# The gated half of the mixers' output projection computed among keys and values, its sums kept in DRAM, the S5 half added in a second pass

## The chip, the core and the metric

The kernel runs on one core of one Trainium2 chip. Its engines work side by side, each through an in-order queue of its own: PE multiplies matrices (PEld loads its weights), DVE and POOL do elementwise work, ACT does copies, casts and functions, and SP issues the DMAs. The metric is the device time of one execution in microseconds (us); lower is better. Everything below is fp32; a product of two fp32 matrices is made of three passes over a high and a low part of each operand.

## What is computed

The reference is one decoder layer on 1024 tokens of width 1024. Its first sub-layer has two mixers whose outputs are laid side by side and go through one output projection, `w_out`; a cross-attention into 256 memory tokens follows:

```python
h = rmsnorm(x, g_mix_pre[l])
s_in, s_gate, g_u, g_vv = jnp.split(h @ w_in[l], splits, axis=-1)
y_ssm = s5_ssm(s_in, ...)
y_ssm = jax.nn.gelu(y_ssm) * jax.nn.sigmoid(s_gate)
y_gmlp = chunked_spatial_gate(g_u, g_vv, g_v[l], w_s[l], b_s[l])
mix = jnp.concatenate([y_ssm, y_gmlp], axis=-1) @ w_out[l]
x = x + rmsnorm(mix, g_mix_post[l])
h = rmsnorm(x, g_x_pre[l])
mem_n = rmsnorm(mem, g_mem[l])
xa = memory_cross_attention(h, mem_n, w_q[l], w_k[l], w_v[l], w_o[l])
```

The S5 mixer (`y_ssm`, rows 0 to 511 of `w_out`) is a scan over time. The gated mixer (`y_gmlp`, rows 512 to 1023) has none and is finished earlier. Keys and values need only the memory tokens. A gated convolutional FFN comes after the attention; the change does not touch it.

## The kernel before

**Tiles.** Activations are held transposed: 128 features on the partitions, and the tokens in two halves `h` of 512. `self.mix[k, h]` is the mixers' output, k = 0 to 3 the S5 half and k = 4 to 7 the gated half; each is a pair of tiles, the high part (a cast by ACT) and the low part (a subtraction by DVE or POOL, `split`, L253/L254). `mm3` (L228) makes one product: for each k-tile three matmuls, high by high, high by low, low by high (all on L234).

**Weights.** A `Stream` holds all weight chunks (128x512, 256 KB) in the order of use. A chunk is loaded into one of 4 `raw` slots (L86), cast by ACT (L132), and its low part is subtracted by DVE (L135); the pair lies in `w`, which has 13 slots, so that some six chunks lie ready ahead of PE.

**The S5 stage.** In `mixers`, the S5 chain runs as a side job beside the matmuls: eight batches, each a passage through PE, DVE, POOL and DMAs that ends in the matmuls of L616/L617, and then `s5_final`, which multiplies with the gate (L657) and splits into `mix[0..3, h]`. When the last batch is still running, PE has the keys (L1043, eight blocks of 24 matmuls 128x256, two weight chunks each) and the values (L1051, four blocks of 48 such matmuls, four chunks each).

**The output projection.** It opens `attention` (L1109): for each token half h and each of 8 output blocks b, `proj` multiplies all eight k-tiles, the gated ones first (24 matmuls 128x512, two weight chunks), ACT copies the sum from PSUM into an `m` tile (L1095), and `sumsq` adds its square (ACT L710, POOL L711). Every weight chunk of `w_out` is loaded and split twice, once for each half. Four PSUM banks, `acc`, take turns.

**What follows.** `post` normalises the eight blocks of a half: the mean square (PE L279, some ten small DVE operations), a broadcast of the factors (PE L306, ACT L309), then for each block the scaling on DVE (L728), the residual on POOL (L729), the high part on ACT (L734) and the low part on DVE (L735). Only then can the queries (`q_block`) use that half. `post` of half 0 runs as a side job beside the projection of half 1; with half 1's projection done, the queries of half 0 come at once. `s_sums`, another side job, prepares weights of the FFN by way of DRAM on POOL and DMAs.

**Order.** The program gives the order and the dependencies; a scheduler that estimates times orders the instructions of each engine when the kernel is built, and each engine then keeps to that order.

Of the kernel before, what the change touches and what calls it, by code (L numbers as in the profile page):

```python
# [19 lines left out]
ALU = mybir.AluOpType  # L20
AX = mybir.AxisListType

P = 128
# [9 lines left out]
W_AHEAD = 6  # L33
PAIR_AHEAD = 12
SUM_AHEAD = 5
ON_POOL = ((4, 16, 1), (164, 184, 2))

POST_A = 0.8
POST_2B = 1
S5_RATE = 1.5  # L40
WARM = 10
EARLY = 1
MIX_AT = 2
# [21 lines left out]
class Stream:  # L65
# [13 lines left out]
    def add(self, ap, pair=None, name=None):  # L79
        self.items.append((ap, pair, name))  # L80
        return len(self.items) - 1
# [71 lines left out]
class Builder:  # L153
# [658 lines left out]
    def prepare(self, cp, dp):  # L812
        nc, a = self.nc, self.a
        g = nc.gpsimd
        self.w = w = Stream(self)

        self.ids = ids = {}

        def add(key, b):
            return [w.add(a[key][b, j]) for j in range(a[key].shape[1])]  # L820

        ids["s01"] = add("w_s01", 0)
        ids["s"] = [add("w_s23", i) for i in range(2)]
        ids["sg"] = [add("w_sg", i) for i in range(4)]
        ids["gv"] = [add("w_gv", i) for i in range(2)]
        ids["gu"] = [add("w_gu", i) for i in range(4)]
        ids["k"] = [add("w_k", i) for i in range(8)]
        ids["v"] = [add("w_v", i) for i in range(4)]
        for n in ("o1", "q", "o2"):
            ids[n] = [[], []]  # L830
        for h in range(2):
            ids["o1"][h] = [add("w_out", i) for i in range(8)]
        for h in range(2):
            ids["q"][h] = [add("w_q", i) for i in range(8)]
            ids["o2"][h] = [add("w_o", i) for i in range(8)]
        ids["up"] = {}
        for i in range(NP):
            ids["up"][i] = [None, None]
        for i in range(NP + 1):
            for j, n in ((0, i), (1, i - 1)):  # L840
                if 0 <= n < NP:
                    ids["up"][n][j] = w.add(a["w_up"][n, j])
        up = {i: {f"{q + 1}{j + 1}": a["w_up"][i + NP * q, j] for q in range(2) for j in range(2)}
              for i in range(NP)}
        raws = {i: {"n": i} for i in up}
        for i in range(-1, NP):
            for d, name in TURN:
                if i + d in up:
                    ids["up"][i + d, name] = w.add(up[i + d], raws[i + d], name)


        self.ones = cp.tile([P, P], F32, name="ones")
        g.memset(self.ones, 1.0)
        first = cp.tile([P, 1], F32, name="first")
        nc.scalar.activation(first, self.ones[:, 0:1], AF.Identity)

        ps = self.bank("st")
        for _ in range(WARM):
            nc.tensor.matmul(ps[:, :P], lhsT=self.ones, rhs=self.ones, start=True, stop=True)
        gains = cp.tile([P, 7, 8], F32, name="gains")  # L860
        self.gain = {n: gains[:, i] for i, n in enumerate(GAINS)}
        self.xs = {}
        for kt in range(KT):
            for h in range(2):
                t = self.slot("m")
                nc.sync.dma_start(t, a["xT"][P * kt:P * kt + P, HALF * h:HALF * h + HALF])
                self.xs[kt, h] = t
                if h == 0 and kt % 2 == 0:
                    w.load_to(kt // 2 + 1)
                if h == 0 and kt == 0:  # L870
                    nc.sync.dma_start(gains, a["gains"])
        self.ident = cp.tile([P, P], F32, name="ident")
        make_identity(nc, self.ident)
        self.conv = cp.tile([P, 44, 4], F32, name="conv")
        self.gv = cp.tile([P, 4], F32, name="gv")

        dram = lambda n, shape: dp.tile(shape, F32, name=n)
        self.ud = [dram(f"ud{i}", [8, P, P]) for i in range(4)]
        self.kd = [dram(f"kd{i}", [240, 64]) for i in range(4)]
        self.yd = [dram(f"yd{i}", [8, 16, 8, P]) for i in range(4)]  # L880
        halves = lambda n, k: [[dram(f"{n}{i}{h}", [P, HALF]) for h in range(2)] for i in range(k)]
        self.gd = halves("gd", 4)
        self.x1d = halves("x1d", 8)
        self.x2d = halves("x2d", 8)
        self.fd = halves("fd", NP)
        self.sd = {n: [dram(f"sd{n}_{i}", [P, HALF]) for i in range(11)] for n in range(1, 5)}
        self.p1d = [dram(f"p1d{i}", [P, HALF]) for i in range(NP)]
        self.v0d = [dram(f"v0d{i}", [P, HALF]) for i in range(NP)]
        self.xg = [[], []]
        self.qscale = [None, None]  # L890
        self.ready = [False, False]
        self.mix = {}


    def mixers(self):
        nc, a, w, ids, xg = self.nc, self.a, self.w, self.ids, self.xg
        v, g = nc.vector, nc.gpsimd
# [4 lines left out]
        for kt in range(KT):  # L902
# [9 lines left out]
            for h in range(2):  # L912
                rh, rl = xg[h][kt]
                for b in range(2):
# [3 lines left out]
                    c = slice(256 * (kt % 2) + P * b, 256 * (kt % 2) + P * b + P)  # L918
# [8 lines left out]
        for b in range(2):  # L927
            for h in range(2):
                t = self.slot("x")
# [110 lines left out]

        memv = lambda k, c=slice(0, 256): tuple(t[:, k % 2, c] for t in self.memp[k // 2])
        self.kraw, self.vraw = [], {}
        for b in range(8):  # L1043
            part = self.blocks(ids["k"][b])
            ps = self.bank()[:, :256]
            self.mm3(ps, [(*part(k), *memv(k)) for k in range(8)], ticks=1)
            if b % 2 == 0:
                self.kraw.append(self.slot("m", shape=[P, 2, 256]))
            nc.scalar.copy(self.kraw[-1][:, b % 2], ps)
        for c in range(4):  # L1050
            part = self.blocks(ids["v"][c], 256)  # L1051
            for mt in range(2):
                ps = self.bank()[:, :256]
                self.mm3(ps, [(*memv(k, slice(P * mt, P * mt + P)), *part(k)) for k in range(8)], ticks=1)
                if c % 2 == 0:
                    self.vraw[mt, c // 2] = self.slot("m")
                nc.scalar.copy(self.vraw[mt, c // 2][:, 256 * (c % 2):256 * (c % 2) + 256], ps)
        self.memp = None
        self.drain(s5)

# [1 line left out]
    def attention(self):  # L1062
# [37 lines left out]

        m1 = [[None] * 8, [None] * 8]
        sq1 = [None, None]
        xres = lambda i, hh: a["xT"][P * i:P * i + P, HALF * hh:HALF * hh + HALF]
        post = [None, None]
        s_job = self.s_sums()
        kv = self.side(kv_parts(), 1)
        for h in range(2):
            for b in range(8):
                proj(lambda k, hh: self.mix[k, hh], "o1", m1, sq1, b, h, (4, 5, 6, 7, 0, 1, 2, 3))  # L1109
                if h == 0:  # L1110
                    next(s_job)
            for k in range(8):
                del self.mix[k, h]
            post[h] = self.post(m1[h], sq1[h], "g_mix_post", xres, h, "q", lambda i, hh: self.x1d[i][hh])
            if h == 0:
                self.drain(kv)
                self.side(post[0])
# [534 lines left out]
```

## Time and profile before

| | |
|---|---|
| median of 3 runs | 1344.74 us (1344.46 to 1349.69) |
| the profiled execution | 1350.66 us, its span 1348.9 us |
| PE busy | 1271.5 us, 94% of the span |
| DVE, POOL, ACT busy | 1072.2, 687.2, 627.9 us |
| mean granted clock of PE | 0.977 |
| keys and values | 265.00 to 331.08 us of the span |
| output projection of the mixers | 331.08 to some 420 us |

The profiled execution took 5.9 us more than the median; all times of single instructions come from it. In a timeline row the columns are start, length, engine, line of the code, operation, output and inputs, the count, and in brackets the idle time before it with what ended it. Line numbers are those of the kernel before; in the changed kernel the same lines stand 3 or 4 further down in the helpers (L135 is L138 there, L617 is L620, L728 is L731, L735 is L738).

### The profile page before, as it was taken

What the parts mean: (1) busy time and instruction counts of PE and PEld (TensorE: products, weight loads), DVE (VectorE), ACT (ScalarE), POOL (GpSimd) and SP (SyncE); (2) the same over time, 40 slices, a digit from 0 to 9 for tenths busy, and PEclk for the clock granted to TensorE, in tenths of its full rate; (3) what the DMA queues carried; (4) which work ended last, traced back from release to release, by engine and by line L of the source; (5) the groups of instructions that cost most, each with busy time, mean ns of one, the idle gap of its engine ahead of it and who ended that gap; (6) DMA issues with size and microseconds to landing.
All of it is one profiled execution on the core that took longest, in us unless ns stands there. A gap on an engine that the chain in (4) does not pass through costs nothing.

```text
span 1348.9 us, 19263 instructions
## 1 busy us (share of the span) xinstructions
PE 1271.5 (94%) x6352; PEld 1077.2 (80%) x6352; DVE 1072.2 (79%) x1628; ACT 627.9 (47%) x1176; POOL 687.2 (51%) x523
## 2 busy tenths in 40 slices
PE   9889999779999899899999999999999999899995
PEld 7769987668888788678887878888888888788885
DVE  7968989886567776996666977988888879966767
ACT  8233421244445444454545645555555555446441
POOL 1685455747544734630443848656565317832235
PEclk9989998899999899999999999999999999999998
DMA  9464435348826962451358566545454359745224
GB/s 312 142 198 118 115 93 165 85 128 314 279 84 214 318 225 88 126 191 57 94 162 283 168 233 223 168 145 164 149 175 154 110 165 389 244 161 176 66 87 156
DMA packets 150660, 233.56 MB, mean 173 GB/s; under 512 B 33696, under 2 KB 43040, under 8 KB 150560
## 3 DMA queue, kind: packets, MB, share of 16 engines
q1 hardware_dynamic: 150560, 232.34, 53.3%
q8 instruction: 49, 0.80, 0.2%
q14 instruction: 51, 0.42, 0.1%
HBM read 174.23 MB, written 53.85 MB: 169 GB/s over the span
## 4 chain that ended last, share of the span: by engine, by line
PE 59%; DVE 10%; DMA 7%; issue 3%; ACT 2%; POOL 1%; SPq 1%; DVEq 0%; ACTq 0%; POOLq 0%
PE acc L234 38%; PE sx L234 17%; DVE w L135 2%; PE st L234 2%; DMA fr<-fd 1%; DMA raw<-in_w_q 1%; DVE m L728 1%; DVE w L254 1%; DMA f<-fd 1%; DVE b L254 1%; PE st L306 1%; DMA raw<-in_w_v 1%; POOL ac L711 1%; ACT w L132 1%; PE st L279 0%
## 5 line engine op out<-in xcount | busy, mean ns | idle before, releaser
L234 PE MATMUL acc<-b,w 128*128 128x512 f32 x2460 | 596.4, 396 | 14.9 <-ACT m L1491 4.1
L234 PEld LDWEIGHTS acc<-b,w 128*128 128x128 f32 x2460 | 464.8, 191 | 115.8 <-ACT m L1491 4.6
L135 DVE TENSOR_TENSOR w<-raw,w 128x512 fp32r<-128x512 f32 x206 | 203.0, 995 | 93.5 <-PE acc L234 40.7
L234 PE MATMUL sx<-b,w 128*128 128x512 f32 x873 | 211.5, 392 | 1.5 <-ACT T L1301 1.5
L132 ACT CAST w<-raw 128x512 fp32r<-128x512 f32 x228 | 141.0, 621 | 132.2 <-PE acc L234 65.7
L234 PEld LDWEIGHTS sx<-b,w 128*128 128x128 f32 x873 | 164.8, 189 | 36.4 <-ACT T L1301 1.9
L711 POOL TENSOR_TENSOR ac<-ac,sq 128x512 f32<-128x512 f32 x45 | 68.9, 1535 | 133.3 <-ACT sq L710 90.3
L234 PE MATMUL acc<-T,w 128*128 128x512 f32 x528 | 127.0, 389 | 0.0
L234 PEld LDWEIGHTS acc<-T,w 128*128 128x128 f32 x528 | 99.1, 188 | 20.6
L254 DVE TENSOR_TENSOR w<-b,w 128x512 fp32r<-128x512 f32 x64 | 67.3, 1059 | 26.5 <-PE st L234 9.5
L1424 POOL TENSOR_TENSOR f<-f,f 128x512 f32<-128x512 f32 x33 | 54.5, 1663 | 48.6 <-DMA f<-fd 48.2
L729 POOL TENSOR_TENSOR m<-m,t 128x512 f32<-128x512 f32 x24 | 40.5, 1717 | 64.9 <-DVE m L728 41.5
L234 PE MATMUL sx<-T,w 128*128 128x512 f32 x264 | 66.5, 389 | 0.0
L254 DVE TENSOR_TENSOR b<-f,b 128x512 fp32r<-128x512 f32 x53 | 55.4, 1060 | 3.5 <-ACT b L253 3.2
L710 ACT ACTIVATE sq<-m 128x512 f32<-128x512 f32 x66 | 41.0, 630 | 36.2 <-DVE ac L711 16.3
L234 PEld LDWEIGHTS sx<-T,w 128*128 128x128 f32 x264 | 49.6, 188 | 10.3
L116 POOL TENSOR_TENSOR st<-st,b 128x512 f32<-128x512 f32 x20 | 27.1, 1353 | 55.9 <-DMA st<-in_w_up 28.3
L253 ACT CAST w<-b 128x512 fp32r<-128x512 f32 x64 | 39.6, 620 | 31.4 <-PE acc L234 18.3
L1240 POOL TENSOR_TENSOR b<-b,m 128x512 f32<-128x512 f32 x22 | 31.3, 1421 | 44.7 <-ACT m L1239 44.7
L135 POOL TENSOR_TENSOR w<-raw,w 128x512 fp32r<-128x512 f32 x22 | 30.1, 1373 | 42.9 <-ACT w L132 24.9
L253 ACT CAST b<-f 128x512 fp32r<-128x512 f32 x53 | 32.7, 620 | 38.1 <-DVE w L254 34.1
L234 PE MATMUL acc<-w,b 128*128 128x256 f32 x384 | 49.3, 285 | 0.0
(356 smaller groups left out, 2330.0 us busy)
## 6 DMA issues: line engine op xcount, KB each, us to landing
raw<-in_w_up SPq DMA_DIRECT2D x68, 256.0 KB, 2.9
f<-fd SPq DMA_DIRECT2D x55, 256.0 KB, 4.6
b<-sd SPq DMA_DIRECT2D x44, 256.0 KB, 4.0
b<-in_w_up SPq DMA_DIRECT2D x40, 256.0 KB, 2.7
raw<-in_w_out SPq DMA_DIRECT2D x32, 256.0 KB, 3.3
raw<-in_w_q SPq DMA_DIRECT2D x32, 256.0 KB, 2.8
raw<-in_w_o SPq DMA_DIRECT2D x32, 256.0 KB, 2.8
m<-in_w_dk SPq DMA_DIRECT2D x28, 256.0 KB, 4.9
```

The source lines that it names most:

```text
L116: g.tensor_tensor(p["S4"], p["12"], p["S2"], ALU.subtract)
L132: nc.scalar.copy(hi[:, :w], t[:, :w])
L135: e.tensor_tensor(lo[:, :w], t[:, :w], hi[:, :w], ALU.subtract)
L234: self.pin(nc.tensor.matmul(ps, lhsT=x, rhs=y, start=first and i + j == 0, stop=last and i == n - 1 and j == 2, skip_group_check=go_on))
L253: self.nc.scalar.copy(hi, src)
L254: (e or self.nc.vector).tensor_tensor(lo, src, hi, ALU.subtract)
L306: self.pin(nc.tensor.matmul(ps[:, i * P:(i + 1) * P], lhsT=r[:, i:i + 1].to_broadcast([P, P]), rhs=self.ident, start=True, stop=True))
L710: nc.scalar.activation(sq, src, AF.Square)
L711: (e or nc.gpsimd).tensor_tensor(acc, acc, sq, ALU.add)
L729: g.tensor_tensor(x, x, rs, ALU.add)
L1240: nc.gpsimd.tensor_tensor(val, val, gate, ALU.mult)
L1424: self.nc.gpsimd.tensor_tensor(s[to], s[x], s[y], ALU.subtract)
```

## The change

`FILL` is a list that sets the order of the stage: keys `k`, values `v` and, new, the gated part of the projection `o1g`, mostly one block of each in turn. An `o1g` block multiplies the four gated k-tiles of both token halves with one weight chunk (2 x 12 matmuls 128x512), ACT copies each sum from PSUM into an `st` tile (3 slots), and a DMA writes it to DRAM (`o1d`). In `attention` the projection keeps the four S5 k-tiles: the partial sum comes back from DRAM into an `m` tile, two blocks ahead, 12 matmuls make the S5 part, and DVE adds it from PSUM (L1132 of the changed kernel) where ACT copied before. The weights of the gated half are now loaded and split once, not twice; `ON_POOL`, which names chunks by number, moves by the eight chunks that go.

```diff
-ON_POOL = ((4, 16, 1), (164, 184, 2))
+ON_POOL = ((4, 16, 1), (156, 176, 2))
...
+FILL = [("k", 0), ("o1g", 0), ("k", 1), ("o1g", 1), ("k", 2), ("o1g", 2), ("k", 3), ("o1g", 3), ("k", 4), ("o1g", 4),
+        ("k", 5), ("o1g", 5), ("k", 6), ("v", 0), ("o1g", 6), ("k", 7), ("v", 1), ("o1g", 7), ("v", 2), ("v", 3)]
...
+        for c, i in FILL:
+            ids[c][i] = [w.add(a["w_out"][i, 1])] if c == "o1g" else add("w_" + c, i)
+        ids["o1s"] = [[w.add(a["w_out"][i, 0]) for i in range(8)] for h in range(2)]
...
-        for b in range(8):
-            part = self.blocks(ids["k"][b])
-            ps = self.bank()[:, :256]
-            self.mm3(ps, [(*part(k), *memv(k)) for k in range(8)], ticks=1)
...
+        for name, b in FILL:
+            part = self.blocks(ids[name][b], 256 if name == "v" else P)
+            if name == "k":
...
+            else:
+                for h in range(2):
+                    ps = self.bank()
+                    self.mm3(ps, [(*part(k), *self.mix[4 + k, h]) for k in range(4)], ticks=1)
+                    t = self.slot("st")
+                    nc.scalar.copy(t, ps)
+                    nc.sync.dma_start(self.o1d[b][h], t)
+        for k in range(4, 8):
+            del self.mix[k, 0], self.mix[k, 1]
...
         for h in range(2):
+            sq1[h] = self.slot("ac")
             for b in range(8):
-                proj(lambda k, hh: self.mix[k, hh], "o1", m1, sq1, b, h, (4, 5, 6, 7, 0, 1, 2, 3))
+                while b + 2 >= n_o1[h] and n_o1[h] < 8:
+                    m1[h][n_o1[h]] = self.slot("m")
+                    nc.sync.dma_start(m1[h][n_o1[h]], self.o1d[n_o1[h]][h])
+                    n_o1[h] += 1
+                part = self.blocks([ids["o1s"][h][b]])
+                ps = self.bank()
+                self.mm3(ps, [(*part(k), *self.mix[k, h]) for k in range(4)], ticks=1)
+                t = m1[h][b]
+                v.tensor_tensor(t, t, ps, ALU.add)
+                self.sumsq(t, sq1[h], b == 0)
```

On PE, DVE, ACT and POOL the order is the same up to the start of the keys, and again from some way into the first attention heads on (row 2,080 of PE's 5,832); SP's loads follow the chunks. Between them three places matter below.

PE at the last S5 batch (L617; L620 in the changed kernel). Rows that read `acc<-m` are keys (`m` the memory tokens), rows `acc<-b` of 128x512 are gated projection; the number behind `w` is the weight chunk. Before:

```order
L234 MATMUL acc<-m_2768,w_3177 128x256
L234 MATMUL acc<-m_2767,w_3178 128x256
L234 MATMUL acc<-m_2793,w_3177 128x256
L234 MATMUL acc<-m_2794,w_3177 128x256
L234 MATMUL acc<-m_2793,w_3178 128x256
L234 MATMUL acc<-m_2793,w_3177 128x256
L234 MATMUL acc<-m_2794,w_3177 128x256
L617 MATMUL sx<-x_1860,x_1901 128x127
L616 MATMUL sx<-x_1808,x_1899 128x128
```

Now:

```order
L237 MATMUL acc<-b_2952,w_2891 128x512
L237 MATMUL acc<-b_2953,w_2891 128x512
L237 MATMUL acc<-b_2952,w_2892 128x512
L237 MATMUL acc<-b_2956,w_2891 128x512
L237 MATMUL acc<-b_2957,w_2891 128x512
L237 MATMUL acc<-b_2956,w_2892 128x512
L237 MATMUL acc<-m_2783,w_2985 128x256
L620 MATMUL sx<-x_1876,x_1917 128x127
L619 MATMUL sx<-x_1824,x_1915 128x128
```

Before, 131 key matmuls stand between the start of the keys and L617; now 49 key matmuls and the 48 of two whole projection blocks do.

DVE at `post` of half 0 (`m` are its blocks, `st` the broadcast factors, L735 or L738 the low parts `b` that the queries read). Before:

```order
L135 TENSOR_TENSOR w_4311<-raw_4177,w_4310 128x512
L135 TENSOR_TENSOR w_4347<-raw_4218,w_4346 128x512
L728 SCALAR_TENSOR_TENSOR m_3689<-m_3689,gains,st_4159 128x512
L728 SCALAR_TENSOR_TENSOR m_3746<-m_3746,gains,st_4159 128x512
L728 SCALAR_TENSOR_TENSOR m_3804<-m_3804,gains,st_4159 128x512
L728 SCALAR_TENSOR_TENSOR m_3862<-m_3862,gains,st_4159 128x512
L728 SCALAR_TENSOR_TENSOR m_3912<-m_3912,gains,st_4159 128x512
L728 SCALAR_TENSOR_TENSOR m_3962<-m_3962,gains,st_4159 128x512
L728 SCALAR_TENSOR_TENSOR m_4012<-m_4012,gains,st_4159 128x512
L135 TENSOR_TENSOR w_4375<-raw_4248,w_4374 128x512
L728 SCALAR_TENSOR_TENSOR m_4062<-m_4062,gains,st_4159 128x512
L735 SCALAR_TENSOR_TENSOR b_4192<-m_3689,gains,b_4191 128x512
```

Now:

```order
L1132 TENSOR_TENSOR m_4363<-m_4363,acc 128x512
L731 SCALAR_TENSOR_TENSOR m_3965<-m_3965,gains,st_4357 128x512
L731 SCALAR_TENSOR_TENSOR m_3967<-m_3967,gains,st_4357 128x512
L731 SCALAR_TENSOR_TENSOR m_3969<-m_3969,gains,st_4357 128x512
L731 SCALAR_TENSOR_TENSOR m_4004<-m_4004,gains,st_4357 128x512
L731 SCALAR_TENSOR_TENSOR m_4041<-m_4041,gains,st_4357 128x512
L731 SCALAR_TENSOR_TENSOR m_4078<-m_4078,gains,st_4357 128x512
L731 SCALAR_TENSOR_TENSOR m_4115<-m_4115,gains,st_4357 128x512
L731 SCALAR_TENSOR_TENSOR m_4152<-m_4152,gains,st_4357 128x512
L138 TENSOR_TENSOR w_4634<-raw_4496,w_4633 128x512
L1132 TENSOR_TENSOR m_4405<-m_4405,acc 128x512
L738 SCALAR_TENSOR_TENSOR b_4397<-m_3965,gains,b_4396 128x512
```

All eight scalings stand in a row in front of the first low part, as before; new in front of it is an addition from PSUM, that of half 1's block 6 (`m_4405`); the one of block 7 comes later.

PE at the end of the projection. The first rows are the last of the projection's block 7, half 1; rows from `b_4191` (before) or `b_4396` (now) on are queries of half 0. Before:

```order
L234 MATMUL acc<-b_3244,w_4460 128x512
L234 MATMUL acc<-b_3245,w_4460 128x512
L234 MATMUL acc<-b_3244,w_4461 128x512
L234 MATMUL acc<-b_4191,w_4502 128x512
L234 MATMUL acc<-b_4192,w_4502 128x512
L234 MATMUL acc<-b_4191,w_4503 128x512
```

Now:

```order
L237 MATMUL acc<-b_3210,w_4457 128x512
L237 MATMUL acc<-b_3211,w_4457 128x512
L237 MATMUL acc<-b_3210,w_4458 128x512
L237 MATMUL acc<-b_4396,w_4492 128x512
L237 MATMUL acc<-b_4396,w_4592 128x512
L237 MATMUL acc<-b_4396,w_4633 128x512
L237 MATMUL acc<-b_4397,w_4492 128x512
```

The queries went block by block; now the first three blocks (chunks `w_4492`, `w_4592`, `w_4633`) go side by side through each tile of the half. Between the broadcast of `post` (L306, L309 now) and the first query matmul stood 126 matmuls of the projection; now 23 do.

More of the change, by code (lines that the diff above doesn't have):

```diff
@@ L826, in prepare @@
         ids["gu"] = [add("w_gu", i) for i in range(4)]
-        ids["k"] = [add("w_k", i) for i in range(8)]
-        ids["v"] = [add("w_v", i) for i in range(4)]
-        for n in ("o1", "q", "o2"):
+        ids["k"], ids["v"], ids["o1g"] = {}, {}, {}
+        for c, i in FILL:
+            ids[c][i] = [w.add(a["w_out"][i, 1])] if c == "o1g" else add("w_" + c, i)
+        ids["o1s"] = [[w.add(a["w_out"][i, 0]) for i in range(8)] for h in range(2)]
+        for n in ("q", "o2"):
             ids[n] = [[], []]
-        for h in range(2):
-            ids["o1"][h] = [add("w_out", i) for i in range(8)]
         for h in range(2):
@@ L1042, in mixers @@
         self.kraw, self.vraw = [], {}
-        for b in range(8):
-            part = self.blocks(ids["k"][b])
-            ps = self.bank()[:, :256]
-            self.mm3(ps, [(*part(k), *memv(k)) for k in range(8)], ticks=1)
[L1047 to L1052, printed above, removed]
-                ps = self.bank()[:, :256]
[L1054 to L1057, printed above, removed]
+        for name, b in FILL:
+            part = self.blocks(ids[name][b], 256 if name == "v" else P)
+            if name == "k":
+                ps = self.bank()[:, :256]
+                self.mm3(ps, [(*part(k), *memv(k)) for k in range(8)], ticks=1)
+                if b % 2 == 0:
+                    self.kraw.append(self.slot("m", shape=[P, 2, 256]))
+                nc.scalar.copy(self.kraw[-1][:, b % 2], ps)
+            elif name == "v":
+                for mt in range(2):
+                    ps = self.bank()[:, :256]
+                    self.mm3(ps, [(*memv(k, slice(P * mt, P * mt + P)), *part(k)) for k in range(8)], ticks=1)
+                    if b % 2 == 0:
+                        self.vraw[mt, b // 2] = self.slot("m")
+                    nc.scalar.copy(self.vraw[mt, b // 2][:, 256 * (b % 2):256 * (b % 2) + 256], ps)
+            else:
[7 more added lines that the diff above has]
+            del self.mix[k, 0], self.mix[k, 1]
         self.memp = None
@@ L1102, in attention @@
         sq1 = [None, None]
+        n_o1 = [0, 0]
         xres = lambda i, hh: a["xT"][P * i:P * i + P, HALF * hh:HALF * hh + HALF]
@@ L1107, in attention @@
         for h in range(2):
+            sq1[h] = self.slot("ac")
             for b in range(8):
-                proj(lambda k, hh: self.mix[k, hh], "o1", m1, sq1, b, h, (4, 5, 6, 7, 0, 1, 2, 3))
+                while b + 2 >= n_o1[h] and n_o1[h] < 8:
[8 more added lines that the diff above has]
+                self.sumsq(t, sq1[h], b == 0)
                 if h == 0:
                     next(s_job)
-            for k in range(8):
+            for k in range(4):
                 del self.mix[k, h]
```

1 line of the change is left out of this document (added).

## The prediction

> **What bounds the kernel now.** I read the page first, then the windows of the stages that the change touches, PE's waits in them, and the timelines of the engines that PE waits for.
>
> ```profile
> PE 1271.5 (94%) x6352; PEld 1077.2 (80%) x6352; DVE 1072.2 (79%) x1628; ACT 627.9 (47%) x1176; POOL 687.2 (51%) x523
> ...
> PE 59%; DVE 10%; DMA 7%; issue 3%; ACT 2%; POOL 1%; SPq 1%; DVEq 0%; ACTq 0%; POOLq 0%
> ```
>
> PE is the bound; only its idle time can be won. The change leaves PE's matmuls as they are in number and shape: it moves 192 of 128x512 forward. So the question is how much PE idles in three stages, in the columns PE, PEld, DVE, ACT, POOL busy, clock, DMA share and GB/s: keys and values, the projection, and the first queries.
>
> ```profile
> 265.00:331.08 66.08, 53.33 (x403) 50.66 (x402) 51.17 (x52) 32.76 (x66) 38.69 (x26) 0.97 0.60 193
> 331.08:419.80 88.72, 88.57 (x397) 73.07 (x398) 54.62 (x64) 42.03 (x75) 47.16 (x31) 1.00 0.60 198
> 419.80:470.00 50.20, 45.35 (x219) 38.82 (x218) 37.60 (x58) 23.40 (x49) 31.73 (x24) 0.93 0.85 288
> ```
>
> Keys and values leave 66.08 - 53.33 = 12.75 us of PE idle, the projection 0.15 us. The waits of PE in the first of these windows say why (total, times, longest):
>
> ```profile
> PE acc L234 <- DVE w L135: 7.0, 7, 2.3
> PE sx L617 <- DVE x L606: 3.8, 1, 3.8
> PE acc L234 <- ACT w L132: 0.9, 2, 0.6
> ```
>
> Weights come late from DVE, because DVE runs the S5 chain at the same time. A key block asks for two chunks in 24 x 0.128 = 3.1 us (66 matmuls in 8.46 us, next fence), a gated block for one chunk in 24 x 0.23 = 5.5 us. That is what the filler can cure.
>
> **The change part by part.** *Filler, up to the last S5 batch.* PE and DVE there:
>
> ```profile
> 265.00 1.48 PE L234 MATMUL acc<-m,w 128*128 128x256 f32 x11
> ...
> 291.98 0.49 PE L617 MATMUL sx<-x,x 128*128 128x127 f32 x2 [3.84 <-DVE x L606]
> ...
> 294.86 8.02 PE L234 MATMUL acc<-m,w 128*128 128x256 f32 x61
> 302.72 8.46 PE L234 MATMUL acc<-w,m 128*128 128x256 f32 x66
> ...
> 331.08 14.12 PE L234 MATMUL acc<-b,w 128*128 128x512 f32 x61 [0.91 <-DVE w L135]
> ...
> 276.62 1.78 DVE L594 TENSOR_TENSOR x<-x,x 128x512 f32<-128x512 f32 x1
> 278.32 1.74 DVE L135 TENSOR_TENSOR w<-raw,w 128x512 fp32r<-128x512 f32 x1
> 279.99 1.77 DVE L595 TENSOR_TENSOR x<-x,x 128x512 f32<-128x512 f32 x1
> 281.68 0.68 DVE L135 TENSOR_TENSOR w<-raw,w 128x512 fp32r<-128x512 f32 x1
> ```
>
> From 265.00 to 291.98 PE runs 131 key matmuls (131 x 0.128 = 16.8 us) and an L616 (0.2); the rest, 26.98 - 17.0 = 10.0 us, is waiting. The new order puts 49 key and 48 gated matmuls there, 49 x 0.128 + 48 x 0.23 = 17.3 us. L617 still waits for L606, and L606 for DVE's chain, which shares its queue with the weight splits. Between L593 and L606 stood eight splits, now five, and one more `mix` split (0.68 us); some of those that go ran in DVE's waits for the DMA, so I count the chain 2 us earlier (0 to 4). PE's idle up to L617 becomes 26.98 - 2 - 17.3 - 0.2 = 7.5 us: 2.5 us are won, not 10.
>
> *Filler, behind it.* The remaining 12.75 - 10.0 = 2.75 us are weight waits among keys and values. With three chunks in 8.6 us of PE and six chunks ahead I leave 0.55 us: 2.2 us are won. All together 4.7 us, between 2.7 (chain no earlier: 0.5 in front of L617, 2.2 behind it) and 12.75 (all idle gone).
>
> *Evictions, stores, loads.* The 16 stores and 16 loads of 256 KB ride on idle DMA (share 0.60) against eight weight loads that go; ACT copies 16 sums in either version. The one transfer near the path is the first load of a partial sum: its `m` slot was the memory tokens', free some 18 matmuls (2.3 us) before the stage ends, its use comes 12 matmuls later (2.8 us), together 5.1 us, and loads of this size land as follows:
>
> ```profile
> f<-fd SPq DMA_DIRECT2D x55, 256.0 KB, 4.6
> ...
> m<-in_w_dk SPq DMA_DIRECT2D x28, 256.0 KB, 4.9
> ```
>
> So it costs 0; if the cover is gone, 1 or 2 us, and four PSUM banks take that up. SP holds loads and stores in one queue: a store that waits for its copy holds the weight loads behind it, but those are for chunks two blocks ahead (over 10 us).
>
> *Second pass.* In 192 x 0.23 = 44 us DVE has 16 splits and 16 additions. The nearest row of an addition from PSUM is L1000, and it runs while POOL is busy:
>
> ```profile
> 258.26 0.68 DVE L1000 TENSOR_TENSOR sq<-acc,st 128x512 f32<-128x512 f32 x1
> ...
> 254.94 4.53 POOL L254 TENSOR_TENSOR b<-m,b 128x512 fp32r<-128x512 f32 x3
> ```
>
> At 0.68 us for an addition and 0.68 to 1.78 for a split DVE needs 22 to 39 us of the 44: hidden, 0.5 us for delays. Were the additions slowed like the splits (1.78), 57 us: 13 us over.
>
> *The junction with the queries.* This is where I expect the loss. `post` of half 0 needs its time, and half 1's projection, which covers it, is now half as long. Its course before:
>
> ```profile
> 390.19 1.05 PE L306 MATMUL st<-ident,rs_y 128*128 128x128 f32 x8
> 391.00 18.44 PE L234 MATMUL acc<-b,w 128*128 128x512 f32 x80
> 409.59 27.12 PE L234 MATMUL acc<-b,w 128*128 128x512 f32 x118 [0.15 <-DVE w L135]
> ...
> 391.98 9.92 DVE L728 SCALAR_TENSOR_TENSOR m<-m,gains,st 128x512 f32<-128x512 f32 x7 [2.12 <-ACT st L309]
> 393.31 8.59 DVE L728 SCALAR_TENSOR_TENSOR m<-m,gains,st 128x512 f32<-128x512 f32 x5
> 401.83 1.77 DVE L135 TENSOR_TENSOR w<-raw,w 128x512 fp32r<-128x512 f32 x1
> 403.52 1.78 DVE L728 SCALAR_TENSOR_TENSOR m<-m,gains,st 128x512 f32<-128x512 f32 x1
> 405.23 0.74 DVE L735 SCALAR_TENSOR_TENSOR b<-m,gains,b 128x512 fp32r<-128x512 f32 x1
> ...
> 392.81 11.94 POOL L729 TENSOR_TENSOR m<-m,t 128x512 f32<-128x512 f32 x7 [3.50 <-DVE m L728]
> ```
>
> (The row at 393.31 shows five of the seven scalings of the row at 391.98 by themselves.) The first low part is ready at 405.97, 15.8 us after the broadcast began (390.19). PE did not notice: 126 matmuls, 29 us, were still to come. Now it has 23. Counted from the broadcast's start: PE is through at 0.81 + 23 x 0.23 = 6.1, and three first query matmuls take 0.7, to 6.8. DVE begins the scalings at 1.8, has done eight at 1.8 + 9.92 + 1.7 = 13.4, then a split (1.77) and the addition that stands there (0.68), and the low part is ready at 16.6, less some 0.2 of overlap: 16.4. PE stands still for 9.6 us. From then on three query blocks go side by side, nine matmuls or 2.1 us a tile, about the pace of the low parts that follow (0.74 each with splits and additions between), so nothing more. Bounds: if the scalings ran at 0.67 us (the first two of the seven did, in 9.92 - 8.59 us; the other five took 1.72), low part at 1.8 + 8 x 0.67 + 0.68 + 0.68 + 0.74 = 9.3, a loss of 2.5; if all eight took 1.72 and split and addition 1.78, 1.8 + 13.8 + 3.6 + 0.7 = 19.9, a loss of 13.1.
>
> *A slow start after the stall.* What PE does after a long gap, beside the same matmuls shortly before:
>
> ```profile
> 437.36 3.13 PE L234 MATMUL sx<-kv,t 128*128 128x256 f32 x24
> ...
> 457.10 4.42 PE L234 MATMUL sx<-kv,t 128*128 128x256 f32 x19 [4.24 <-DVE t L254]
> ```
>
> 0.130 us each before, 0.233 after 4.24 us of idle: 19 x 0.10 = 2.0 us lost. I add 2.0 (0 to 2.8). After the gap of 3.84 us at L617 the 61 matmuls ran at 8.02 / 61 = 0.131, not slower.
> The Trainium skill (TensorE: Matmul & The Clock Gate, Part 1) speaks against a change that opens such a gap: after an idle window of some 3.4 us the clock falls to half, and some 3.4 us of work bring it back. By that page the estimate is 1.7 us in place of 2.0, and a gap of 3.84 us could have cost too, which the trace doesn't show.
>
> *Sum.* -4.7 + 0 + 0.5 + 9.6 + 2.0 = +7.4 us. Against the profiled execution's 1350.66 that is 1358.1; the median of the runs lies 5.9 us lower, so 1344.74 + 7.4 = **1352 us**. Behind the first heads the order is unchanged, and PE's delay is carried to the end: the 50.20 - 45.35 = 4.85 us of idle in the third window hang on softmax behind the same `post` and move with it. I give them 0, with 2 us to either side.
>
> **The rivals.** *A, the fill wins.* Splits out of DVE's queue let the S5 chain run ahead, and the three side-by-side query blocks hide `post`, because POOL's residuals (L729) don't meet the scalings. It decides at 0.67 us a scaling: the junction costs 2.5 us and no slow start, the fill brings up to 12.75. Result -10 to -2 us, at the middle -6.5: 1338. For it speaks that PE's wait is named for weights in 7.0 of 12.75 us; against it that five of seven scalings took 1.72 us, since POOL works in step with them, and nothing in the change parts them.
>
> *B, a tie.* Both effects are as I say but of one size: the chain comes 4 us earlier (fill 6.7), low parts follow after some 13 us (loss 6.2), no slow start. -4.7 - 2 + 6.2 + 0.5 = 0: 1345. For it speaks that the lengths near the junction vary with POOL's work, against it that each of the three must fall on the good side.
>
> *C, DVE bounds the second pass.* If additions cost like splits, PE waits for PSUM banks in the second pass: up to +13 less the slack of four banks (11 us), some 2 to 6 us on top of the forecast, and the addition in front of the low part 1.1 more: +10 to +15, 1357. Against it the row of L1000.
>
> **How the numbers follow.** A measurement can tell about 0.5% (6.7 us) from no change: faster is below 1338.0, slower above 1351.5. Forecast: 0.57, with its own range +1 to +13 (1346 to 1358), as its terms can't all fall to one side; half of it or a little more lies above +6.7: slower 0.30, same 0.27. A 0.14: two thirds beyond -6.7, where the fill is near its upper bound (0.09), else same (0.05). B 0.16, all same. C 0.13, all slower. Faster 0.09, same 0.48, slower 0.43. The range leaves out most of A and the end of C: 1341 to 1360.
>
> **What would show it.** In the changed profile: PE waiting for L609 (the old L606) for 4 us or more in spite of the filler, and hardly any wait for a split behind it; a projection of some 45 us with additions (L1132) of 0.7 us; one idle stretch of PE of 9 to 10 us in front of the first query matmuls, released by DVE L738 or L1132, with slow matmuls behind it; the last low part some 8 us later against the queries than before. It would be wrong if that stretch is under 3 us (then A), if keys, values and filler together leave PE idle for over 12 us (the fill wins nothing), or if L1132 takes 1.7 us (then C).

## The result and the profile after

The changed kernel took 1356.3 us (median of 6 runs, 1351.73 to 1359.35) against 1346.52 us for the kernel before, run beside it (6 runs, 1344.46 to 1349.69): a ratio of 1.0058, interval 1.0039 to 1.0078. Slower, by about 8 us. A second time, beside the experiments, it was 1.0062 (1.0038 to 1.0086). The profiled execution took 1357.33 us, its span is 1355.5 us.

The page's first part, of the changed kernel: PE's busy time grew by 3.5 us with the same 6352 matmuls, so some of them ran slower.

```profile
PE 1275.0 (94%) x6352; PEld 1079.4 (80%) x6352; DVE 1077.7 (80%) x1636; ACT 627.2 (46%) x1168; POOL 682.9 (50%) x523
```

The windows of the changed kernel from the first key matmul to the projection, and from there to the first scores (length, then PE, PEld, DVE, ACT, POOL busy, clock, DMA share, GB/s):

```profile
264.69:371.72 107.03, 97.60 (x593) 87.45 (x592) 60.14 (x63) 48.28 (x91) 53.29 (x36) 0.95 0.74 252
371.72:447.45 75.73, 66.65 (x292) 54.54 (x291) 58.30 (x71) 34.67 (x59) 42.13 (x27) 0.93 0.54 182
```

Before, the first of these was 66.08 us without the gated matmuls; with 192 x 0.227 = 43.6 us for them it is 109.7. So keys, values and filler together win 2.65 us. The second was 106.28 us (331.08 to 437.36) with the gated matmuls, 62.7 without: 13.1 us are lost there (12.9 up to the start of the first scores, which is at 447.29). PE's timeline of the changed kernel:

```profile
271.74 0.50 PE L237 MATMUL acc<-b,w 128*128 128x512 f32 x1 [1.51 <-ACT b L256]
...
290.31 0.79 PE L620 MATMUL sx<-x,x 128*128 128x127 f32 x2 [4.59 <-DVE x L609]
...
293.38 3.93 PE L237 MATMUL acc<-m,w 128*128 128x256 f32 x23
...
352.67 1.38 PE L237 MATMUL acc<-b,w 128*128 128x512 f32 x4 [1.96 <-ACT w L135]
...
411.01 1.05 PE L309 MATMUL st<-ident,rs_y 128*128 128x128 f32 x8
411.82 5.95 PE L237 MATMUL acc<-b,w 128*128 128x512 f32 x25
426.56 0.80 PE L237 MATMUL acc<-b,w 128*128 128x512 f32 x1 [8.79 <-DVE m L1132]
427.64 19.81 PE L237 MATMUL acc<-b,w 128*128 128x512 f32 x77 [0.28 <-DVE b L738]
...
465.82 3.09 PE L237 MATMUL sx<-kv,t 128*128 128x256 f32 x14 [2.01 <-DVE t L257]
```

In order: a wait for the casts of the gated mixer's output that the forecast did not have; the old wait for the S5 chain, still 4.59 us; a wait for a weight's cast ahead of the last gated block; and, after 25 matmuls behind the broadcast (L309), 8.79 + 0.28 us in which PE stands still at the first queries, with 77 matmuls of 0.257 us behind it in place of 0.23. What DVE and POOL do in that gap:

```profile
412.72 11.52 DVE L731 SCALAR_TENSOR_TENSOR m<-m,gains,st 128x512 f32<-128x512 f32 x8 [0.62 <-ACT st L312]
424.16 1.75 DVE L138 TENSOR_TENSOR w<-raw,w 128x512 fp32r<-128x512 f32 x1
425.83 0.67 DVE L1132 TENSOR_TENSOR m<-m,acc 128x512 f32<-128x512 f32 x1
426.43 1.16 DVE L738 SCALAR_TENSOR_TENSOR b<-m,gains,b 128x512 fp32r<-128x512 f32 x1
...
413.56 11.80 POOL L732 TENSOR_TENSOR m<-m,t 128x512 f32<-128x512 f32 x7 [3.62 <-DVE m L731]
```

Eight scalings take 1.44 us each, in step with POOL's residual additions; the first low part is ready at 427.59, 16.6 us after the broadcast began. From the first scores to the first transposes (L1183) the changed kernel then takes 2.5 us less than before: the wait of 4.24 us there is down to 2.01, and eight query matmuls, 1.8 us, that stood behind the start of the first scores now stand ahead of it (from the broadcast on, 103 - 23 = 80 of them against 198 - 126 = 72). The matmuls behind the wait are slow here too: 14 took 3.09 us, at a granted clock of 0.56 from 465.82 to 468.71. Against the kernel before, the changed one is late by -0.3 us at the first key, -3.0 at the projection (the gated matmuls counted in on both sides), +9.9 at the first scores, +7.4 at the first transposes and +6.6 at the end of the span.

### The profile page after: what moved, and what is told of

Read it like the earlier page. It is cut to its first block, busy times and chain, and to the rows that moved or that the text cites. A ratio compares the mean times of both kernels' runs of the same rounds, so it can differ in the third digit from the quotient of the medians.

```text
span 1355.5 us, 19337 instructions
## 1 busy us (share of the span) xinstructions
PE 1275.0 (94%) x6352; PEld 1079.4 (80%) x6352; DVE 1077.7 (80%) x1636; ACT 627.2 (46%) x1168; POOL 682.9 (50%) x523
## 4 chain that ended last, share of the span: by engine, by line
PE 48%; DVE 4%; DMA 1%; ACT 1%; issue 1%; POOL 0%; SPq 0%; DVEq 0%; ACTq 0%; POOLq 0%
PE acc L237 28%; PE sx L237 17%; PE st L237 2%; DVE m L731 1%; DMA rs<-x1d 1%; DVE w L138 1%; DVE m L786 0%; PE st L309 0%; DVE m L788 0%; DMA p1d<-t 0%; PE st L282 0%; DVE ac L1564 0%; DVE m L777 0%; POOL m L732 0%; DVE rs_t L267 0%
## 5 line engine op out<-in xcount | busy, mean ns | idle before, releaser
L237 PE MATMUL acc<-b,w 128*128 128x512 f32 x2460 | 604.3, 398 | 26.3 <-DVE m L1132 8.8
L138 DVE TENSOR_TENSOR w<-raw,w 128x512 fp32r<-128x512 f32 x198 | 194.0, 987 | 107.6 <-PE acc L237 49.2
L135 ACT CAST w<-raw 128x512 fp32r<-128x512 f32 x220 | 136.6, 622 | 128.3 <-PE acc L237 82.2
L1448 POOL TENSOR_TENSOR f<-f,f 128x512 f32<-128x512 f32 x33 | 51.7, 1578 | 50.9 <-DMA f<-fd 50.4
L256 ACT CAST w<-b 128x512 fp32r<-128x512 f32 x64 | 39.4, 619 | 26.4 <-PE acc L237 16.4
```

The lines of the kernel that those rows point to most:

```text
L135: nc.scalar.copy(hi[:, :w], t[:, :w])
L138: e.tensor_tensor(lo[:, :w], t[:, :w], hi[:, :w], ALU.subtract)
L237: self.pin(nc.tensor.matmul(ps, lhsT=x, rhs=y, start=first and i + j == 0, stop=last and i == n - 1 and j == 2, skip_group_check=go_on))
L256: self.nc.scalar.copy(hi, src)
L1448: self.nc.gpsimd.tensor_tensor(s[to], s[x], s[y], ALU.subtract)
```

## The experiments

The theory at first was the prediction's sum: the fill wins some 5 us, the junction with the queries takes some 11, the way through DRAM costs next to nothing. The rivals put the cost into the partial sums' way through DRAM and the additions, or held that whatever is spared at one place is lost at another. Each time below stands against runs of the kernel before that were made beside it; 0.001 of the ratio is 1.35 us. The runs e4, e9, e11 and e6 leave out a part of the computation; all others compute the whole layer.

| run | edit of the changed kernel | ratio | interval |
|---|---|---|---|
| e1_half0 | only half 0's gated part forward | 1.0036 | 1.0020 to 1.0052 |
| e7_half1 | only half 1's | 1.0136 | 1.0115 to 1.0156 |
| e2_fill_last | gated blocks behind the values | 1.0079 | 1.0058 to 1.0101 |
| e4_no_dram | no stores, loads, additions | 0.9997 | 0.9984 to 1.0010 |
| after_again | none | 1.0062 | 1.0038 to 1.0086 |
| e9_adds_only | no stores, no loads | 1.0011 | 0.9993 to 1.0028 |
| e11_no_stores | no stores | 1.0021 | 1.0004 to 1.0038 |
| e6_no_residual | no residual for half 0 | 0.9999 | 0.9982 to 1.0016 |
| e12_half1_in_part | half 1: four blocks of eight forward | 1.0076 | 1.0060 to 1.0093 |
| e16_sums_later | FFN weight sums moved behind | 1.0118 | 1.0095 to 1.0140 |
| e13_both | e12 and e16 together | 1.0015 | 1.0000 to 1.0030 |
| e17_both_sums_near | e12, sums beside half 1's projection | 1.0041 | 1.0025 to 1.0057 |

### One half forward, then the other

```diff
-        ids["o1s"] = [[w.add(a["w_out"][i, 0]) for i in range(8)] for h in range(2)]
+        ids["o1s"] = [[w.add(a["w_out"][i, 0]) for i in range(8)]]
+        ids["o1"] = [[], [add("w_out", i) for i in range(8)]]
...
-                for h in range(2):
+                for h in range(1):
```

> Only half 0 of the gated projection is made among keys and values and goes by way of DRAM; half 1 is projected as before, all eight k-tiles in one pass, so that the cover of half 0's norm is 24 matmuls a block again. If the loss sits at the junction with the queries (theory), the stall of 9 us there and the slow matmuls behind it are gone, while most of the fill stays: 3 to 6 us less than the kernel before, some 12 less than the changed one. If the way through DRAM, the copies and the additions cost it (rival), half of them are left and half of the loss: 3 to 5 us more than the kernel before.

> The same amount of filler, stores, loads and additions, but for half 1; half 0 is projected in one pass. Half 1's second pass, which covers half 0's norm, stays short. Theory: the stall of some 9 us before the first queries stays, and the result is 5 to 10 us over the kernel before. Rival (DRAM, copies, additions): the same time as with half 0 in DRAM, within 2 us.

Both move the same number of matmuls, stores and additions; they differ in which projection stands between half 0's sums and the first queries, 43.6 us of it in e1 and 21.8 in e7. They lie 1.0% apart. PE of e7, where the gap is as in the changed kernel:

```profile
435.60 0.80 PE L237 MATMUL acc<-b,w 128*128 128x512 f32 x1 [8.98 <-DVE m L1138]
```

In e1 there is no gap at that place. From the first key to the projection both take the same, 93.92 us in e1 and 94.18 in e7; from there to the first scores e1 takes 88.17 us and e7 98.81. So 10.6 us of the distance lie where the theory had them, at the junction. The times themselves are not the theory's: e1 came out at the rival's number, not at -3 to -6 us, and e7 is some 18 us over the kernel before where 5 to 10 were expected. PE of e1 among the values, and the window there:

```profile
340.99 0.50 PE L237 MATMUL acc<-w,m 128*128 128x256 f32 x2 [1.20 <-ACT w L135]
...
357.28 0.73 PE L237 MATMUL acc<-b,w 128*128 128x512 f32 x2 [1.31 <-ACT w L135]
...
330.00:360.00 30.00, 22.08 (x134) 18.09 (x133) 14.11 (x12) 11.77 (x23) 20.32 (x14) 0.97 1.04 391
```

Thirteen such waits, from 331 to 367 us, make 8.4 us (in an execution of 1359.31 us, 6.6 above the median of e1): weights come late while the DMA engines are full. A gated block for one half asks for a weight chunk per 12 matmuls, in the changed kernel per 24. So the junction is worth what the theory said, and a cost showed up that it did not have.

### The gated blocks in one piece behind the values

```diff
-FILL = [("k", 0), ("o1g", 0), ("k", 1), ("o1g", 1), ...
+FILL = [("k", i) for i in range(8)] + [("v", i) for i in range(4)] + [("o1g", i) for i in range(8)]
```

> The order of the stage is changed back: all keys, all values, then the gated projection in one piece; two passes, DRAM and additions stay. Theory: PE's idle among keys and values is back to 12 to 13 us, and the kernel is 3 to 5 us slower than the changed one, some 12 over the kernel before, with the junction's stall unchanged at 9 us. Rival: the fill wins nothing, same time as the changed kernel within 2 us.

PE of this kernel (its lines stand one lower):

```profile
275.81 2.54 PE L236 MATMUL acc<-m,w 128*128 128x256 f32 x12 [2.87 <-DVE w L137]
...
291.04 0.80 PE L619 MATMUL sx<-x,x 128*128 128x127 f32 x2 [3.83 <-DVE x L608]
...
428.23 0.79 PE L236 MATMUL acc<-b,w 128*128 128x512 f32 x1 [8.80 <-DVE m L1131]
```

The waits for splits among the keys are back, the S5 batch comes at 291.04 (290.31 in the changed kernel), the gap at the queries stays. The interleaving by itself is worth 0.002, some 2 to 3 us, and the intervals overlap: this lies between the theory's 3 to 5 us and the rival's under 2, and decides for neither. Why it is so little comes below.

### Nothing through DRAM

```diff
-                    nc.sync.dma_start(self.o1d[b][h], t)
...
-                while b + 2 >= n_o1[h] and n_o1[h] < 8:
-                    m1[h][n_o1[h]] = self.slot("m")
-                    nc.sync.dma_start(m1[h][n_o1[h]], self.o1d[n_o1[h]][h])
-                    n_o1[h] += 1
...
-                t = m1[h][b]
-                v.tensor_tensor(t, t, ps, ALU.add)
+                t = m1[h][b] = self.slot("m")
+                nc.scalar.copy(t, ps)
```

> Leaves out the 16 stores, the 16 loads and the additions: the gated half is computed and copied out of PSUM but not added; ACT copies the S5 sums out of PSUM as in the kernel before. Theory: the stall before the queries is still 8 to 9 us, and the time is that of the changed kernel less 0 to 2 us. Rival: it comes back to the kernel before, some 8 us less than the changed one.

The theory missed and the rival's number came: 0.0061 of the ratio, 8 us, against 0 to 2. PE's stretch at the queries in this run:

```profile
420.70 20.13 PE L237 MATMUL acc<-b,w 128*128 128x512 f32 x77 [8.16 <-DVE b L738]
```

The gap is there as before, so the 8 us lie elsewhere. The next runs take the way through DRAM apart, with the changed kernel run again beside them.

### Stores, loads and additions one by one

The run with additions alone takes the tile of the block before as the other operand (block 0 is copied); the one without stores loads rows of x:

```diff
-                    nc.sync.dma_start(self.o1d[b][h], t)
...
-                    nc.sync.dma_start(m1[h][n_o1[h]], self.o1d[n_o1[h]][h])
+                    nc.sync.dma_start(m1[h][n_o1[h]], xres(n_o1[h], h))
```

> The changed kernel itself, beside the next three on one chip, so that they can be set against it. Both theories: 1.0058 of the kernel before, give or take 0.002.

> Leaves out the 16 stores and the 16 loads of the gated half's sums; each of the 16 additions on VectorE stays, but takes the tile before it in place of the gated half's sum, so that part of the computation is left out. In the run that had neither the way through DRAM nor the additions the time was 0.9997 of the kernel before, 8 us under the changed kernel. Theory (the transfers cost it: the stores and loads hold up weights and their casts): without them the additions cost nothing, 0.999 to 1.001. Rival (the additions cost it, being 16 x 0.67 us more on VectorE just ahead of the stall at the queries): 1.004 to 1.006.

> Leaves out the 16 stores of the gated half's sums alone; the 16 loads stay, but fetch rows of the input x, which the additions take, so the gated half's part of the sum is left out. Theory (the transfers): if it is the stores that cost, 0.999 to 1.002, near the run without any of the way; if it is the loads, 1.004 to 1.006, as the changed kernel. Rival (the additions): 1.004 to 1.006 as well, but then the run with additions alone stands there too.

Additions alone leave 1.0011, loads with them 1.0021, both a ten-thousandth above the theory's ranges; these two steps are within their intervals. The stores make the step from 1.0021 to 1.0062, 5.5 us (the two intervals together allow 1.6 to 9.5). The windows from the first key to the projection, in turn the changed kernel again, without stores, additions alone:

```profile
264.17:373.79 109.62, 97.62 (x593) 87.42 (x592) 58.69 (x64) 47.68 (x92) 53.16 (x37) 0.97 0.73 246
```

```profile
264.32:366.90 102.58, 95.92 (x593) 87.25 (x592) 60.52 (x64) 47.91 (x91) 54.49 (x36) 0.97 0.66 221
```

```profile
262.70:365.42 102.72, 95.71 (x594) 87.07 (x593) 60.87 (x64) 48.34 (x92) 55.26 (x37) 0.97 0.64 216
```

Against 109.7 before, the fill wins 7.1 us there, and the stores take all of it back in this execution of the changed kernel (4.4 us of it in the one shown first). Where: PE of the changed kernel again, then the casts on ACT, then the stretch in a window, and the same stretch without stores.

```profile
346.62 3.54 PE L237 MATMUL acc<-w,m 128*128 128x256 f32 x25 [1.12 <-DVE w L138]
...
356.71 5.73 PE L237 MATMUL acc<-b,w 128*128 128x512 f32 x24 [3.43 <-ACT w L135]
```

```profile
331.08 0.59 ACT L1067 COPY st<-acc 128x512 f32<-128x512 f32 x1 [2.24 <-DMA o1d<-st]
334.79 0.62 ACT L135 CAST w<-raw 128x512 fp32r<-128x512 f32 x1 [3.12 <-DMA raw<-in_w_out]
...
344.44 0.62 ACT L135 CAST w<-raw 128x512 fp32r<-128x512 f32 x1 [3.79 <-DMA raw<-in_w_v]
```

```profile
330.00:360.00 30.00, 24.44 (x157) 21.46 (x156) 9.01 (x11) 11.96 (x23) 16.69 (x13) 1.00 0.98 363
```

```profile
330.00:360.00 30.00, 30.00 (x209) 28.09 (x209) 13.29 (x16) 14.81 (x30) 14.36 (x10) 1.00 0.84 300
```

PE idles 5.6 us of 30 with the DMA engines 98% busy, and not at all at 84%. Two readings were left: ACT waits for loads because the DMA engines are full, or because a copy ahead of the cast waits for a store to free its slot (the 2.24 us). The run that moves the sums decides on the second, below.

### Without half 0's residual

```diff
-            g.tensor_tensor(x, x, rs, ALU.add)
+            if (mode, h) != ("q", 0):
+                g.tensor_tensor(x, x, rs, ALU.add)
```

> Leaves out half 0's eight additions of the residual on GpSimd in the norm behind the projection, so that the eight scalings on VectorE have no GpSimd work beside them. Theory (the stall before the first queries is as long as it is because scalings at 1.44 us each run beside residual additions at 1.69): scalings of 0.67 us, the first low part some 6 us sooner, the stall of 9.1 us down to 2 to 4, no slow clock behind it: 8 to 10 us off, 0.998 to 1.001. Rival (the stall is set by something else in the chain, the broadcast or the weights' splits on VectorE): the stall stays over 6 us and the gain is under 4 us, 1.003 to 1.006.

DVE and PE of this run:

```profile
414.91 6.44 DVE L731 SCALAR_TENSOR_TENSOR m<-m,gains,st 128x512 f32<-128x512 f32 x8 [0.62 <-ACT st L312]
...
422.66 18.24 PE L237 MATMUL acc<-b,w 128*128 128x512 f32 x79 [2.71 <-DVE b L739]
```

Scalings of 0.80 us, a gap of 2.71, matmuls of 0.231 us behind it, and 0.0063 or 8.5 us off the changed kernel: 6.4 us of gap and some 2.3 us of slow clock (77 matmuls at 0.253 us and one at 0.80 in the changed kernel run again) account for it. Keys and values took as long as in the changed kernel (264.56 to 373.91). The theory of the junction holds to its numbers: POOL's residual additions beside DVE's scalings make 6.4 of the 9.1 us by which the norm outlasts the shortened projection. The Trainium skill (SBUF — State Buffer, SBUF: two separate sides) says why they run in step: a DVE operation with two inputs from SBUF and a GpSimd operation that reads SBUF take a shared pair of ports in turn. The trace agrees: the scalings take 1.44 us beside POOL, 0.80 without, while the additions with one input from PSUM (L1132) keep to 0.67 in the same stretch.

### Four blocks of half 1 in one pass

```diff
-                for h in range(2):
+                for h in range(2 if b < 4 else 1):
...
+                if h == 1 and b > 3:
+                    proj(lambda k, hh: self.mix[k, hh], "o1", m1, sq1, b, h, (4, 5, 6, 7, 0, 1, 2, 3))
+                    continue
```

> Half 0 as in the changed kernel; of half 1 only the first four of eight output tiles have their gated half among the keys and values, the last four are projected in one pass. That puts 48 more matmuls, 48 x 0.227 = 10.9 us, between half 0's last addition and the first queries, and takes 4 of the 16 stores and loads away. Theory (the changed kernel loses 11 us at the first queries, 9 of waiting and 2 of slow clock, because half 1's projection no longer covers half 0's norm): the stall is gone, 9 to 12 us off the changed kernel, 0.997 to 1.000 of the kernel before. Rival (as where half 1 was projected in one pass throughout: the time lost moves to the weights of the values, which come late): 1.002 to 1.005.

Neither number came (the run is over the rival's 1.005 too), but what the rival described did. PE of this run, first among the values, then at the queries:

```profile
342.97 0.50 PE L237 MATMUL acc<-w,m 128*128 128x256 f32 x2 [1.64 <-ACT w L135]
...
409.75 18.21 PE L237 MATMUL acc<-b,w 128*128 128x512 f32 x78
428.27 0.96 PE L237 MATMUL acc<-b,w 128*128 128x512 f32 x3 [0.30 <-DVE b L738]
...
467.35 4.42 PE L237 MATMUL sx<-kv,t 128*128 128x256 f32 x19 [5.17 <-DVE t L257]
```

The gap is gone, as the theory said; four waits of 0.27 to 1.32 us are left there. But from the first key to the projection the run takes 104.3 us with 48 matmuls (10.9 us) fewer, 5.6 us more than the changed kernel run again would with the same count (109.62 - 10.9) and 8.2 more than the execution shown first, for late weights; and the scores wait 5.17 us for softmax, as they did before the change (4.24). What the gap had cost is paid at two other places.

### The sums of the FFN's weights moved

```diff
-                if h == 0:
-                    next(s_job)
...
+                next(s_job, None)
                 if i > 1:
                     next(s_job, None)
...
-                    if i:
-                        next(s_job, None)
+                    next(s_job, None)
...
-                    t[o, j] = self.slot("t" if k < 4 else "m")
+                    t[o, j] = self.slot("m")
```

> The changed kernel, with the sums of the down projection's weights (16 loads and 16 stores of 256 KB that run among the keys and values) moved to the queries stage; nothing is left out. Theory (without the 16 stores of the gated sums the time is 5.5 us less because the 16 DMA engines are 96 to 98% busy from 300 to 360 us and the weights of the last gated tiles and of the values come late): with 8 MB less to move there the engines have room, the waits of 2.3 to 5.5 us for casts and splits of weights ahead of the S5 pass vanish, 1.001 to 1.004 of the kernel before, if the sums cost nothing in their later place. Rival (ScalarE waits for a store to free its slot, and the casts behind it are late for that, however full the DMA engines are): the waits stay, 1.005 to 1.008. The stall at the first queries stays in both.

Among keys and values the theory's number came; in the whole the run is slower than theory and rival had it. The window there, and one in the queries:

```profile
264.12:366.80 102.68, 95.48 (x593) 86.48 (x592) 55.82 (x63) 48.21 (x91) 30.81 (x20) 0.97 0.58 181
...
470.00:520.00 50.00, 46.99 (x230) 38.47 (x229) 34.33 (x49) 19.56 (x43) 33.07 (x24) 0.93 0.95 331
```

All 16 stores are made, and the stage is as short as without them (102.68 against 102.58 us): it was not the store slots. That the full DMA engines delay the weights is not shown by this, because the run takes the sums' 32 transfers out of SP's queue as well. The trace of the changed kernel run again speaks for that queue. The first row below, a split, frees the slot of the load in the last row:

```profile
345.09 1.47 DVE L138 TENSOR_TENSOR w<-raw,w 128x512 fp32r<-128x512 f32 x1 [4.47 <-PE acc L237]
...
345.09 0.33 SPq L89 DMA_DIRECT2D raw<-in_w_v  x1
...
350.28 0.50 SPq L89 DMA_DIRECT2D raw<-in_w_out  x1
```

The slot is free at 346.56 and the load is issued at 350.28, after seven transfers of the sums, the residual and the gated half; PE then waits 3.43 us for its cast. All weight loads from 329 to 354 us leave SP 1.9 to 9.9 us after their slot was free and land 5.1 to 5.7 us later. In the kernel before, with the DMA engines 94% busy, they leave after 0.3 to 2.1 us and land after 3.8 to 5.5; in e16 they leave after 0.03 us. So most of the lateness builds up before the load is issued. SP makes an issue every 0.65 us there; whether that is its own pace or that of the full engines was not tried.

In their later place the sums fill the engines again (95% from 470 to 520 us, 73% in the changed kernel) and the norm behind the attention's projection comes late (its broadcast at 536.94 us, 531.91 in the changed kernel run again); by then the 7 us gained are lost and 5 more. Which of the sums' DMAs and POOL additions does that was not tried.

### Both edits, and the sums nearer

> The two edits of the two runs above together; nothing is left out. Theory: both costs of the changed kernel go, the 11 us at the first queries and some 4 us of late weights, and what is left is the fill's gain of 5 to 7 us: 0.993 to 0.997 of the kernel before. Rival (the time lost shows up elsewhere, behind late weights or the sums in their later place): 0.999 to 1.003.

> As the run with both edits, but the sums of the down projection's weights go beside half 1's projection instead of the queries; nothing is left out. Theory (the DMA engines are full between 300 and 360 us and have room from 360 to 430; in the queries the sums got in the way of other work): most of the late weights' cost goes (about 4 of 6 us), the stall at the first queries stays covered, and nothing is lost behind: 0.996 to 0.9995 of the kernel before. Rival (the sums' additions on GpSimd now stand among those of half 0's norm and hold up the first queries, or too few of the transfers move): 1.001 to 1.005.

e13 puts the two edits above together; e17 keeps the first, and calls the sums in half 1's blocks:

```diff
-                if h == 0:
-                    next(s_job)
+                if h == 1:
+                    next(s_job)
```

PE of e13 at the projection and the first scores:

```profile
358.33 29.66 PE L237 MATMUL acc<-b,w 128*128 128x512 f32 x130
...
435.98 3.13 PE L237 MATMUL sx<-kv,t 128*128 128x256 f32 x24
```

With 91.8 us to the projection (102.7 with the 48 matmuls) and only short waits behind it, e13 is at the scores 1.4 us before the kernel before (437.36) and 11.3 before the changed one. It ends 0.0015 behind the kernel before: the rival's number. At the broadcast behind the attention's projection it is 0.8 us late (523.96 against 523.13), so 2.2 us are lost from the scores to there, where the sums now are, and about as much behind; what loses them was not taken apart. Against the changed kernel it gains 0.0047 (0.0019 to 0.0075). In e17 the sums' loads still go out between 311 and 353 us (312 to 335 in the changed kernel run again), because SP's queue runs ahead of PE; the stage takes 101.0 us (111.9 with the 48 matmuls), and the time is the rival's too. No version that computes the whole layer beat the kernel before.

## Why the prediction was right, and where its sum was not

The sign, the place of the loss and the total came out: +7.4 us forecast; the ratio says +7.8, the medians lie 9.8 us apart, the profiled executions 6.7, and at the first transposes the trace stands at +7.4. Term by term:

- *Junction.* Forecast 9.6 us of standing still, low part 16.4 us after the broadcast's start; measured 8.79 + 0.28 and 16.6. e6 shows the cause, e7 and e1 the place.
- *Slow start.* Forecast 2.0 us; 77 x (0.257 - 0.23) = 2.1, and 0.6 for the one matmul of 0.80 us ahead of them.
- *Second pass.* Forecast 0.5; the additions took 0.67 to 0.69 us and 130 matmuls ran in 29.66 us without a wait: 0. Rival C fell with that.
- *Stores.* "The 16 stores and 16 loads of 256 KB ride on idle DMA (share 0.60)": this step failed. The share was a mean over 66 us. The kernel before in the stretch that counts, there the first third of its projection:

```profile
330.00:360.00 30.00, 29.09 (x129) 23.95 (x128) 14.48 (x12) 12.97 (x25) 24.59 (x18) 1.00 0.94 344
```

  It stood at 0.94 already. The stores cost 4.4 to 7.0 us ahead of the projection and 5.5 us in all. The prediction also held that a weight load behind a store in SP's queue has over 10 us to spare; with loads that left up to 9.9 us late and landed after 5.1 to 5.7, it had not.
- *Filler.* Forecast 4.7 us. Without the stores it wins 7.1, with them 2.65 and 0.1 in two executions (the sign given for a fill that wins nothing, over 12 us of idle time there, was reached but not passed in the second: 109.62 - 97.62 = 12.0). Up to the last S5 batch, with the forecast's prices for the matmuls, it won 1.9 and 0.5 us of the 2.5 forecast, since the batch came 1.4 and 0 us earlier in place of 2. The new wait for the casts of the gated output (1.51 and 0.81 us) is not the reason, because PE still waits 4.59 or 2.74 us for L609 behind it; what holds DVE's chain was not taken apart. Behind the batch, it won 5.7 without stores (7.1 less 1.4 ahead of it) where the forecast had 2.2 of 2.75 us of idle time. Some 2 us of the rest lie in the price of a key matmul: without stores 24 of them take 2.87 us between gated blocks, 0.120 each, while the forecast's 0.128 divides the length of a row, which runs on 0.17 us past the start of the next and holds some slower matmuls; 61 + 192 of them stand behind the batch. The start of one row and of the next, without stores:

```profile
310.51 3.04 PE L237 MATMUL acc<-m,w 128*128 128x256 f32 x24
313.38 5.63 PE L237 MATMUL acc<-b,w 128*128 128x512 f32 x24
```

- *The queries.* Given 0 with 2 us to either side. From the projection to the first transposes the trace loses 10.4 us; less 9.1 of standing still and 2.1 of slow start this leaves -0.8. (The two parts, +1.9 up to the end of the queries ahead of the scores and -2.7 behind, hold the eight query matmuls that changed places.)

So the mechanism of the loss was right and sized to within 0.5 us, while ahead of it a gain too small by 2.4 us and a cost left out of some 5.5 cancelled in part. That was luck: the total was right for a better reason at the junction than in the stage ahead of it.

## What to carry to other kernels

A transfer's cover is the DMA share in the stretch where it runs, not in the stage: look at it in windows of some 30 us before calling a transfer free, and look how long loads stand in the issuing queue after their slot is free. Work that is moved forward leaves its old place, where it may have been the cover of a norm or a softmax: count what is left to run beside that. And where two stages share full engines or a full queue, a cure at one place is paid at the next, so it has to be timed in the whole.

## What the runs showed of the hardware

The clock after a gap of PE, first from the runs' rows at the last S5 batch. After 2.74 us of waiting the pairs of L620 took 0.39 us and 23 key matmuls 2.99; after 3.84 to 3.87 us the pairs took 0.57 to 0.64 and the 23 took 3.14 to 3.65; after 4.59 us, 0.63 and 3.93. In the kernel before, whose gap was 3.84 us, the pairs took the longer time too, and only the 61 matmuls behind them ran at the full pace:

```profile
292.64 0.39 PE L620 MATMUL sx<-x,x 128*128 128x127 f32 x2
```

```profile
292.83 0.64 PE L617 MATMUL sx<-x,x 128*128 128x127 f32 x2
```

(The first is of the changed kernel run again, the second of the kernel before.) So the prediction's remark that the gap of 3.84 us cost nothing looked at the wrong rows: from the first L617 to the keys it took 2.88 us, after the gap of 2.74 us 2.31. The rule of the Trainium skill (TensorE: Matmul & The Clock Gate, Part 1: The HAM clock gate), a window of some 3.4 us of idle time, lies between the two gaps. As the length of one unbroken gap, however, the traces don't bear it out. In the changed kernel run again a wait of 2.89 us, one matmul and a wait of 0.81 were followed by 17 key matmuls in 3.83 us, at a granted clock of 0.50. In e2 a single wait of 2.87 us was followed by 12 in 2.54 us, where the kernel before took 1.70 after 2.29. In the changed kernel the 14 score matmuls came at a clock of 0.56 after waits of 0.36 and 2.01 us. So a gap of two to three microseconds, or several short ones, can bring the slow clock too; 2.74 us without it is no safe length.
